# Weighting expert results out of PSUM and storing them in two halves, in a two-layer backbone with 32 experts

## The chip, the core and the metric

One core of one Trainium2 chip. Its engines are TensorE (PE, with weight loads listed apart as PEld), VectorE (DVE), ScalarE (ACT), GpSimd (POOL) and SyncE (SP, which only issues transfers here); 16 DMA engines move data between HBM and SBUF. Each engine executes its own list of instructions in order and waits on semaphores. The metric is the device time of one execution in microseconds, the median of several.

## The reference

Two layers on 256 latent and 256 context tokens of 1024 channels. Each layer has one input projection, three token mixers, a merge and a normalisation, and then a mixture of 32 experts, the part that is changed here. In layer 0 it works on all 512 tokens, in layer 1 on the 256 latent ones.

```python
weights = softmax(top_logit, -1) * group_w          # 2 experts of 32 for each token
def run_block(args):                                # one expert e, some of its tokens
    tok, e = args
    xb = h_pad[tok]
    return (silu(xb @ w1[e]) * (xb @ w3[e])) @ w2[e]    # w1, w3: 1024 x 512, w2: 512 x 1024
y = lax.map(run_block, ...).reshape(cap, d) * slot_w[:, None]
moe = zeros((n_tok + 1, d)).at[slot_tok].add(y)[:n_tok]     # two results for each token
xl = layer_norm(ALPHA * xl + g2_l * moe, ln2_g, ln2_b)      # g2: one row for latent, one for context
```

## The kernel before

A layer's MoE stage has these steps, all written out by the program; only the size of an expert's group of tokens is known at run time.

*Routing and permuting.* Scores, the two experts of each token, its weights `wgt` and its slot `pos` among all slots sorted by expert are computed on DVE, ACT and POOL. `posi` is the slot's row in the DRAM buffer `ysD`, which has two regions: even experts write region 0, odd ones region 1 (NR = 2). `permute(q)` (L1538) builds one-hot matrices `on` for 256 slots (L1544 on DVE and POOL by turns, L1545 on DVE) and PE multiplies the tokens by them (L1551), which gives `XS`, the tokens in slot order, evacuated by DVE (L1555) and ACT (L1557). There are 4 such quarters in layer 0 and 2 in layer 1. Meanwhile POOL scales the residual `X` by the rows of the first normalisation (L1562), which lie in a part of XS that is not used yet.

*Experts.* A block is 64 slots (RB) of one expert. `expert_steps` (L1597) copies the slots to `xt` (L1610), multiplies by w1 and w3 (L1616), takes silu and product (L1621, L1622), transposes (`turn`, L1627), multiplies by w2 (L1636), evacuates 64 slots x 1024 columns, laid out as 128 partitions x 512, to `yo` on ACT (L1638), and POOL stores that with one transfer to ysD (L1639). Expert 0 stands first, between permute(0) and the others: the blocks of its slots 64 to 255 in a nest of three Ifs (L1664), then its slots 0 to 63, then the other permutes, and in layer 0 a loop for more than 256 slots behind an If (L1693). Then experts 1 to 31 follow (L1701 to L1727), software-pipelined: the gate of e stands before the first half of e + 1's up projection. Behind each expert stands an If for over 64 slots (L1721), which holds one block and, in a nested If (L1724), a loop for over 128 slots (L1725); an expert with 64 slots or fewer jumps over both.

*Weights.* Each expert's 6.3 MB come as six pieces of 1 MB on SP's queue into rings (`fetch`, `load_piece`, `reload`). reload(e) at the end of expert e asks for the pieces that take the places of e's own.

*Finish.* POOL gathers the two result rows of each token from ysD (L1738), 8 gathers of 128 rows in layer 0 and 4 in layer 1. ACT multiplies one by its weight (L1742), DVE adds the other with its weight (L1745), POOL (DVE for the last group) multiplies by the gate g2 (L1746), DVE adds ALPHA times the residual (L1747); `normalise` follows for each pair of groups, in layer 1 also the affine part (L387, L388) and the output. Of the weight pieces of layer 1's input projection that are loaded at that time (`raw`), three are issued on ACT behind the third group's scaling (`late`), the rest on SP.

## Time and profile before

| what | value |
|---|---|
| timed runs | 2794.46, 2794.48 and 2802.67 us, median 2794.48 |
| the profiled execution's own time | 2788.21 us |
| its span | 2786.6 us |
| mean granted PE clock | 0.905 of full speed |
| PE busy | 2209.7 us (79%) |
| DVE busy | 1158.0 us (42%) |
| ACT, POOL busy | 664.0 us (24%), 612.6 us (22%) |
| moved by DMA | 657.22 MB, 236 GB/s over the span |
| MoE stage of layer 0, of layer 1 | about 886 to 1538 us, about 2180 to 2787 us |

The profile shows one execution. Busy shares are means over stages with different limits, so a stage is read from windows and from the instructions at its ends, not from the shares of the whole span. The bytes of the two MoE stages are mostly weights: 32 experts of 6.3 MB in each layer.

### The profile page before, as it was taken

To read this page: it belongs to the slowest core of one execution; us is meant where nothing else is said; L and a number is where in the kernel's file an instruction comes from. 1 tells how busy PE (TensorE), PEld (TensorE's weight loads), DVE (VectorE), ACT (ScalarE), POOL (GpSimd) and SP (SyncE) were. 2 spreads that over 40 slices of the span, in tenths; PEclk is the share of its full clock that TensorE was granted. 3 is DMA by queue.
4 is the path that set the end of the run, shared out by engine and by line. 5 is a ranking of instruction groups with operands and counts; after the bars stand their busy time and mean duration, and the time that the engine had idled before them with its cause. 6 is when DMAs were issued, how large, how long until landed. Compare 5 with 4: busy or idle time off the path is not lost. (4 is left out here: it accounts for less than half of the span.)

```text
span 2786.6 us, 42100 instructions
## 1 busy us (share of the span) xinstructions
PE 2209.7 (79%) x16239; PEld 1551.1 (56%) x16239; DVE 1158.0 (42%) x2451; ACT 664.0 (24%) x1308; POOL 612.6 (22%) x542
## 2 busy tenths in 40 slices
PE   7998988888898887777773899986878687678773
PEld 3666975677685644334331576874777443344331
DVE  4749445876456100000003779467864300000002
ACT  2421345443422100000001342345433100000000
POOL 1242110544333000000002242223554200000001
PEclk9998999999999999899887899998988898898886
DMA  9475451323765488999996258343357769999994
GB/s 316 153 215 171 130 167 42 100 76 103 206 213 197 176 345 318 362 408 408 353 382 219 62 164 262 112 154 87 92 167 241 291 248 381 352 400 408 407 389 157
DMA packets 350438, 657.22 MB, mean 236 GB/s; under 512 B 73462, under 2 KB 253214, under 8 KB 306808
## 3 DMA queue, kind: packets, MB, share of 16 engines
q1 hardware_dynamic: 287890, 599.97, 59.4%
q0 software_dynamic: 38160, 24.63, 2.9%
q10 hardware_dynamic: 24022, 27.84, 2.9%
q8 instruction: 218, 3.57, 0.5%
q14 instruction: 148, 1.21, 0.1%
HBM read 593.09 MB, written 59.02 MB: 234 GB/s over the span
## 5 line engine op out<-in xcount | busy, mean ns | idle before, releaser
L1616 PE MATMUL ps<-we,xt 128*64 128x256 f32 x4224 | 569.6, 423 | 240.5 <-PEq L1721 147.4
L1616 PEld LDWEIGHTS ps<-we,xt 128*64 128x64 f32 x4224 | 339.0, 152 | 458.2 <-issue 329.0
L209 PE MATMUL ps<-hT,whi 128*128 128x512 f32 (+2 forms) x880 | 327.1, 372 | 2.1 <-ACT whi L152 1.9
L154 POOL TENSOR_TENSOR wlo<-raw,whi 128x1024 fp32r<-128x1024 f32 (+1 forms) x84 | 206.2, 2455 | 543.6 <-ACT whi L152 453.2
L211 PE MATMUL ps<-hT,wlo 128*128 128x512 f32 (+2 forms) x880 | 317.2, 360 | 0.3 <-DVE wlo L154 0.3
L210 PE MATMUL ps<-hT,whi 128*128 128x512 f32 (+2 forms) x880 | 317.3, 361 | 0.0
L1639 POOL DMA_DIRECT2D ysD<-yo x69 | 55.6, 806 | 1074.7 <-ACT yo L1638 954.0
L1636 PE MATMUL ps<-we,hh 128*64 128x512 f32 x1104 | 251.9, 597 | 5.2 <-DVE hh L1628 2.6
L152 ACT ACTIVATE whi<-raw 128x1024 fp32r<-128x1024 f32 x174 | 180.1, 1044 | 221.9 <-PE ps L210 158.9
L1638 ACT ACTIVATE yo<-ps 128x512 f32<-128x512 f32 x69 | 41.2, 597 | 798.7 <-PE ps L1636 769.9
L1610 DVE COPY xt<-XS 128x512 f32 x66 | 28.2, 427 | 483.2 <-PE ps L1616 479.0
L1628 DVE COPY hh<-ps 128x256 f32<-128x256 f32 x69 | 29.3, 425 | 409.7 <-PE ps L110 409.7
L209 PEld LDWEIGHTS ps<-hT,whi 128*128 128x128 f32 (+1 forms) x880 | 172.0, 195 | 42.4 <-issue 12.6
L211 PEld LDWEIGHTS ps<-hT,wlo 128*128 128x128 f32 (+1 forms) x880 | 171.4, 195 | 31.4 <-issue 6.9
L210 PEld LDWEIGHTS ps<-hT,whi 128*128 128x128 f32 (+1 forms) x880 | 171.9, 195 | 25.0 <-issue 3.3
L154 DVE TENSOR_TENSOR wlo<-raw,whi 128x1024 fp32r<-128x1024 f32 x90 | 148.1, 1647 | 44.6 <-ACT whi L152 38.8
L1636 PEld LDWEIGHTS ps<-we,hh 128*64 128x64 f32 x1104 | 79.5, 138 | 135.2 <-issue 118.8
L210 PE MATMUL ps<-wlo,hT 128*128 128x256 f32 x384 | 110.1, 287 | 1.5 <-DVE wlo L154 1.5
L209 PE MATMUL ps<-whi,hT 128*128 128x256 f32 x384 | 110.9, 289 | 0.0
L211 PE MATMUL ps<-whi,hT 128*128 128x256 f32 x384 | 109.7, 286 | 0.0
L288 PE MATMUL ps<-wmod,sT 128*32 128x256 f32 x768 | 90.0, 521 | 14.0 <-DMA wmod<-in_w_mod 11.5
L1621 ACT ACTIVATE hd<-ps 128x256 f32<-128x256 f32 x69 | 26.4, 383 | 249.9 <-PE ps L1616 249.9
(423 smaller groups left out, 3718.6 us busy)
## 6 DMA issues: line engine op xcount, KB each, us to landing
we<-in_w SPq DMA_DIRECT2D x338, 1024.0 KB
raw<-in_w_in SPq DMA_DIRECT2D x121, 512.0 KB
wmod<-in_w_mod SPq DMA_DIRECT2D x96, 512.0 KB
we<-in_w SPq DMA_DIRECT2D x92, 512.0 KB
ysD<-yo POOLq DMA_DIRECT2D x69, 256.0 KB, 16.2
ysD<-X SPq DMA_DIRECT2D x17, 512.0 KB
raw<-in_w_out SPq DMA_DIRECT2D x16, 512.0 KB
mgD<-st ACTq DMA_DIRECT2D x24, 256.0 KB
```

Of the source, the lines that this page charges most:

```text
L152: nc.scalar.activation(hr[:, :, off:off + pn], rv, AF.Copy)
L154: eng.tensor_sub(lr[:, :, off:off + pn], rv, hr[:, :, off:off + pn])
L209: mm(ps, st[0](k), mv[0](k), start=(k == 0), stop=False)
L210: mm(ps, st[0](k), mv[1](k), start=False, stop=False)
L211: mm(ps, st[1](k), mv[0](k), start=False, stop=(k == kt - 1))
L288: mm(hold["ps"][32 * j:32 * j + 32, :], sT[:, k, :], cols, start=(k == 0), stop=(k == KD - 1 and v not in mod_d[l]))
L1610: nc.vector.tensor_copy(t["xt"], XS[:, :, ds(off, RB)])
L1616: mm(t["ph"][grp[g], i], t["xt"][:, k], (w1, w3)[i](k, g * 256, 256), start=(k == 0), stop=(k == KD - 1), tile_position=(0, g * RB))
L1628: nc.vector.tensor_copy(tl["hh"], pt)
L1636: mm(py[grp[g]], tl["hh"][:, j, grp[f]], w2(k, g * 512, 512), start=(k == 0), stop=(k == 3), tile_position=(0, g * RB))
L1638: nc.scalar.activation(tl["yo"], py, AF.Copy)
L1639: nc.gpsimd.dma_start(ysD[e % NR, ds(off, RB)].rearrange("s (g c) -> g s c", g=2), tl["yo"])
```

## The change

- The result of a block leaves PSUM on DVE, multiplied by the slot's weight (`wc`, one column, two in layer 0: one for each stream) and by the gate row g2; in layer 0 the two streams' products are added. The ACT copy goes.
- The weights of the slots are scattered in slot order to a DRAM buffer `wsD`, with one indirect transfer on POOL for each of the 2 x nb columns (8 in layer 0, 4 in layer 1), and loaded for each block into `wc` by two transfers of 64 rows on POOL, one expert ahead.
- A block's result is stored by two transfers of 64 rows x 512 columns (on POOL, for the last expert on ACT).
- Slots 64 to 127 of an expert are a straight block behind one If. Slots beyond 127 of all experts go to one loop behind one If (`rare`), which stands behind expert 0 in both layers.
- At the end the gathered rows are added to X by plain DVE additions; ALPHA is multiplied into the rows of the first normalisation before (POOL). `normalise` follows all additions.
- The `late` loads are issued on SP with the others. g2 is loaded at the stage's start. The one-hot tiles of permute are single ones in a ring of nb + nst, written in place; hd and hh share a tile.

```diff
-            if late["n"]:
-                late["n"] -= 1
-                with tc.issue_after(late["ins"]):
-                    nc.scalar.dma_start(dst, v)
-            else:
-                nc.sync.dma_start(dst, v)
+            nc.sync.dma_start(dst, v)
...
+        nst = len(streams)
+        wsD = dram.tile([ns + RB, nst], F32, name=f"wsD{l}")
+        g2 = [pe.tile([P, 512], F32, name=f"g2_{s}") for s in streams]
+        for i, s in enumerate(streams):
+            for g in range(2):
+                nc.sync.dma_start(g2[i][g * RB:(g + 1) * RB], mod_d[l][5][s, g * 512:(g + 1) * 512].partition_broadcast(RB))
...
-            on = pr.tile([P, nb, QT], F32R, name="on", tag="on", bufs=2)
+            on = [pr.tile([P, QT], F32R, name="on", tag="on", bufs=nb + nst) for _ in range(nb)]
...
+        nc.gpsimd.tensor_scalar(lnrow, lnrow, ALPHA, None, op0=OP.mult)
...
+        wgt = pr.tile([P, 2, nb, nst], F32, name="wgt")
+        nc.gpsimd.memset(wgt, 0.0)
...
+        nc.scalar.dma_start(wsD[ns:ns + RB], XS[0:RB, 0, ns:ns + nst])
+        for i in range(2):
+            for b in range(nb):
+                nc.gpsimd.indirect_dma_start(out=wsD, out_offset=bass.IndirectOffsetOnAxis(ap=posw[:, i, b:b + 1], axis=0),
+                                             in_=wgt[:, i, b], in_offset=None)
...
+            def weights():
+                for g in range(2):
+                    nc.gpsimd.dma_start(tl["wc"][grp[g]], wsD[ds(off, RB)])
...
-                nc.scalar.activation(tl["yo"], py, AF.Copy)
-                nc.gpsimd.dma_start(ysD[e % NR, ds(off, RB)].rearrange("s (g c) -> g s c", g=2), tl["yo"])
+                for x in range(nst):
+                    nc.vector.scalar_tensor_tensor(tl["hd" if x else "yo"], py, tl["wc"][:, x:x + 1], g2[x], op0=OP.mult,
+                                                   op1=OP.mult)
+                if nst > 1:
+                    nc.vector.tensor_add(tl["yo"], tl["yo"], tl["hd"])
+                last = isinstance(e, int) and e == NE - 1
+                for g in range(2):
+                    (nc.scalar if last else nc.gpsimd).dma_start(ysD[region, ds(off, RB), g * 512:(g + 1) * 512],
+                                                                 tl["yo"][grp[g]])
...
-            with ExitStack() as deeper:
-                for off in range(RB, QT, RB):
-                    deeper.enter_context(tc.If(cnt > off))
-                    expert_block(to, 0, off)
+            with tc.If(cnt > RB):
+                expert_block(to, 0, RB)
...
+        top = nc.values_load(cmax_i, min_val=0, max_val=nt, skip_runtime_bounds_check_because=WHY)
+        with tc.If(top > 2 * RB, label=f"rare{l}", preferred_fallthrough_block=True):
+            with tc.For_i(0, NE, NR) as e0:
+                for x in range(NR):
...
+                    with tc.If(cnt > 2 * RB):
+                        with tc.For_i(2 * RB, cnt, RB) as i:
+                            expert_block(block_tiles(px, *ZO), e, more(off + i), streamed(e), x)
...
+        steps[1][5]()
         steps[1][0]()
...
+                nx[5]()
                 nx[0]()
...
             with tc.If(cnt > RB, label=f"beyond{l}_{e}", preferred_fallthrough_block=True):
-                to = block_tiles(px, *ZO)
-                expert_block(to, e, more(off + RB))
-                with tc.If(cnt > 2 * RB):
-                    with tc.For_i(2 * RB, cnt, RB) as i:
-                        expert_block(to, e, more(off + i))
+                expert_block(block_tiles(px, *ZO), e, more(off + RB))
...
-        g2 = mod_rows(pf, l, 5, streams)
...
-            y0, y1 = yg[b, 0], yg[b, 1]
-            ins = nc.scalar.activation(y0, y0, AF.Copy, scale=wgt[:, 0, b:b + 1])
-            if b == 2:
-                late["ins"] = ins.ins
-            nc.vector.scalar_tensor_tensor(y0, y1, wgt[:, 1, b:b + 1], y0, op0=OP.mult, op1=OP.add)
-            (nc.vector if b == nb - 1 else nc.gpsimd).tensor_mul(y0, y0, g2[(b0 + b) // 2])
-            nc.vector.scalar_tensor_tensor(X[:, b0 + b], X[:, b0 + b], ALPHA, y0, op0=OP.mult, op1=OP.add)
-            if b % 2:
-                normalise([b0 + b - 1, b0 + b])
+            for i in range(2):
+                nc.vector.tensor_add(X[:, b0 + b], X[:, b0 + b], yg[b, i])
+        for b in range(0, nb, 2):
+            normalise([b0 + b, b0 + b + 1])
```

## Rows read from the trace of the kernel before

**Rows 1.** groups by form: the up projection (count, busy, mean ns, idle before, releasers)

```profile
L1616 PE MATMUL ps<-we,xt 128*64 128x256 f32 x4224 | 569.6, 423 | 240.5 <-PEq L1721 147.4 <-DMA we<-in_w 60.4 <-DVE xt L1610 13.9
```

**Rows 2.** line views of L1721, L1693, L1664: branches (count, ns min/median/max, first and last start)

```profile
...
L1721 PEldq COMPARE_BRANCH  x62: 70/3387/7289, 966.8 to 2738.4; - x62
...
L1721 DVEq COMPARE_BRANCH  x62: 50/56/63, 971.1 to 2737.9; - x62
...
L1693 PEldq COMPARE_BRANCH  x1: 362/362/362, 947.2 to 947.2; - x1
...
L1664 PEldq COMPARE_BRANCH  x4: 86/1897/3735, 899.7 to 2190.5; - x4
...
```

**Rows 3.** windows: stretch, length, busy of each engine (instructions), PE clock, DMA share, GB/s

```profile
1066.40:1176.42 110.02, 78.47 (x498) 40.94 (x496) 7.57 (x18) 5.88 (x12) 4.79 (x7) 0.86 0.95 368
1189.26:1303.97 114.71, 85.84 (x578) 45.23 (x576) 8.83 (x21) 6.86 (x14) 5.57 (x7) 0.91 1.02 408
1057.75:1480.05 422.30, 312.60 (x2030) 163.60 (x2032) 30.26 (x72) 24.12 (x49) 19.93 (x26) 0.88 0.97 382
2297.97:2725.00 427.03, 321.14 (x2087) 170.21 (x2084) 31.96 (x76) 24.89 (x51) 20.72 (x26) 0.88 0.99 390
```

**Rows 4.** timeline, end of layer 0's stage (start, us, engine, line, operation, idle before)

```profile
...
1490.22 0.80 POOL L1639 DMA_DIRECT2D ysD<-yo  x1 [9.38 <-ACTq L1721]
...
1500.40 1.07 POOL L1738 DMA_INDIRECT yg<-ysD,posi  x1 [9.38 <-issue]
...
1509.43 0.94 POOL L1738 DMA_INDIRECT yg<-ysD,posi  x1 [0.30 <-issue]
...
1514.96 6.65 DVE L1747 SCALAR_TENSOR_TENSOR X<-X,yg 128x1024 f32<-128x1024 f32 x2
...
1519.27 0.37 ACTq L166 DMA_DIRECT2D raw<-in_w_in  x1
...
1538.07 3.93 PE L110 MATMUL ps<-cst,X 128*128 128x128 f32 x16 [48.83 <-DVE X L384]
...
```

**Rows 5.** timeline, end of layer 1's stage

```profile
...
2743.85 0.80 POOL L1639 DMA_DIRECT2D ysD<-yo  x1 [10.70 <-ACTq L1721]
...
2755.74 1.05 POOL L1738 DMA_INDIRECT yg<-ysD,posi  x1 [11.10 <-DMA ysD<-yo]
...
2773.46 0.21 DVE L378 BATCH_NORM_AGGREGATE bmv<-bst 128x2 f32<-128x12 f32 x1
...
```

**Rows 6.** line views of L1639 and L1738 (landing); transfers of 2735 to 2787, 40 slices

```profile
L1639 POOL DMA_DIRECT2D ysD<-yo x69: 796/796/1077, 913.6 to 2743.8; - x69
...
DMA to landing us min/median/max: 8.6/16.2/21.2
...
DMA to landing us min/median/max: 4.3/5.7/6.5
...
DMA  1012001889711110069988400000000000007920
```

**Rows 7.** timeline of POOL and DVE around expert 0 of both layers

```profile
...
855.06 18.61 POOL L1562 TENSOR_TENSOR X<-X,XS 128x1024 f32<-128x1024 f32 x8 [7.44 <-DMA XS<-in_ln_g]
...
891.53 0.15 DVE L1589 TENSOR_TENSOR wgt<-wgt,e 128x4 f32<-128x4 f32 x1
...
920.94 0.42 DVE L1622 TENSOR_TENSOR hd<-hd,ps 128x256 f32<-128x256 f32 x1 [4.53 <-ACT hd L1621]
...
2188.46 9.30 POOL L1562 TENSOR_TENSOR X<-X,XS 128x1024 f32<-128x1024 f32 x4 [0.61 <-DVE wgt L1588]
...
2211.27 0.69 DVE L1555 COPY XS<-ps 128x512 f32<-128x512 f32 x1 [5.96 <-PE ps L1551]
...
```

**Rows 8.** windows: layer 0 behind expert 0

```profile
935.00:985.00 50.00, 44.79 (x347) 32.20 (x345) 8.20 (x17) 4.69 (x9) 2.61 (x3) 0.97 0.49 190
```

**Rows 9.** groups by form: prices on DVE and POOL

```profile
L1746 DVE TENSOR_TENSOR yg<-yg,mrow 128x1024 f32<-128x1024 f32 x2 | 2.4, 1210 | 0.0
...
L1544 POOL TENSOR_SCALAR o<-io,posq 128x256 f32<-128x256 f32 x10 | 10.1, 1005 | 47.6 <-DVE o L1544 21.4 <-DVE posq L1536 13.7 <-DVE on L1545 11.1
```

More of the change, by code (lines that the diff above doesn't have):

```diff
@@ L156, in split_unit @@
         return hr, lr
-    late = {"n": 0, "ins": None}
     def col_load(src, c0, cn):
@@ L416, in backbone @@
         nq = T - q0
-        late["n"] = 3 if l else 0
         yD = [dram.tile([HID, T], F32, name=f"yD{l}_{i}") for i in range(3)]
@@ L1427, in backbone @@
         cnt_i = pe.tile([1, 2, NE], I32, name="cnt_i")
+        cmax = pe.tile([1, 1], F32, name="cmax")
+        cmax_i = pe.tile([1, 1], I32, name="cmax_i")
+        one_i = pe.tile([1, 2, 1], I32, name="one_i")
         def block_pool(stack, bufs):
@@ L1463, in backbone @@
                    tile_position=(0, 64 * (k % 2)))
-            ls_ = pr.tile([P, CTX], F32, name="ls", tag="o1", bufs=2)
+            ls_ = pr.tile([P, CTX], F32, name="ls", tag="on", bufs=nb + nst)
             nc.vector.tensor_copy(ls_, lT)
@@ L1528, in backbone @@
         nc.vector.tensor_copy(cnt_i, cs_[0:1])
+        nc.vector.tensor_reduce(cmax, cs_[0:1, 0], axis=AX.X, op=OP.max)
+        nc.vector.tensor_copy(cmax_i, cmax)
         pall = pr.tile([P, nb, NE], F32, name="pall", tag="eq", bufs=2)
@@ L1550, in permute @@
                         for x in range(2):
-                            mm(ps[:, i], h2r[(b0 + b) // 2, kp + i][x][:, b % 2], on[:, b], start=(b == 0 and x == 0),
+                            mm(ps[:, i], h2r[(b0 + b) // 2, kp + i][x][:, b % 2], on[b], start=(b == 0 and x == 0),
                                stop=(b == nb - 1 and x == 1))
@@ L1576, in backbone @@
             nc.vector.tensor_add(posi[:, i], pos[:, i], rofs)
+        posw = pr.tile([P, 2, nb], I32, name="posw")
+        nc.vector.tensor_copy(posw, pos)
+        wgt = pr.tile([P, 2, nb, nst], F32, name="wgt")
+        nc.gpsimd.memset(wgt, 0.0)
+        own = [wgt[:, i, 2 * x:2 * x + 2, x] for i in range(2) for x in range(nst)]
         eg = pr.tile([P, nb, NG], F32, name="eg")
@@ L1635, in down @@
                         for g in range(2):
-                            mm(py[grp[g]], tl["hh"][:, j, grp[f]], w2(k, g * 512, 512), start=(k == 0), stop=(k == 3),
+                            mm(py[grp[g]], hh[:, j, grp[f]], w2(k, g * 512, 512), start=(k == 0), stop=(k == 3),
                                tile_position=(0, g * RB))
-                nc.scalar.activation(tl["yo"], py, AF.Copy)
-                nc.gpsimd.dma_start(ysD[e % NR, ds(off, RB)].rearrange("s (g c) -> g s c", g=2), tl["yo"])
-            return rows, up, gate, turn, down
+                for x in range(nst):
+                    nc.vector.scalar_tensor_tensor(tl["hd" if x else "yo"], py, tl["wc"][:, x:x + 1], g2[x], op0=OP.mult,
[6 more added lines that the diff above has]
+                                                                 tl["yo"][grp[g]])
+            return rows, up, gate, turn, down, weights
         def expert_block(*args):
-            rows, up, gate, turn, down = expert_steps(*args)
+            rows, up, gate, turn, down, weights = expert_steps(*args)
+            weights()
             rows()
@@ L1705, in backbone @@
         for e in range(1, NE):
-            rows, up, gate, turn, down = steps.pop(e)
+            rows, up, gate, turn, down, _ = steps.pop(e)
             tc.mark_branch_hint_location(f"beyond{l}_{e}", "LikelyTaken")
```

36 lines of the change are left out of this document (19 added, 17 removed).

## The prediction

> **What bounds the kernel now.** I read four views in this order. The groups of instructions by form first: the costliest group is the up projection of the experts (L1616), and the releaser in front of its idle time is not the weights but PE's own sequencer at L1721, the jump over the second block of an expert: 147.4 of 240.5 us, against 60.4 us for weights that had not landed [rows 1]. Then the line view of L1721: PE meets that branch 62 times, with 70 ns, 3.39 us and 7.29 us as minimum, median and maximum; on DVE the same branch takes 50 to 63 ns. So it is neither the register nor the count that makes it long, but something that PE alone does at that jump [rows 2]. The nearest rows of the same kind are PE's L1693, a jump over a loop that holds one block (0.362 us), and L1664, whose jump over three nested blocks in layer 1 took 3.735 us, its maximum [rows 2].
>
> Third, windows cut at the stores of single experts. 1066.40 to 1176.42 is six experts, and the branch was long in each: 110.02 / 6 = 18.34 us an expert, PE busy 78.47, DMA share 0.95 at 368 GB/s. 1189.26 to 1303.97 is seven experts behind which the branch was short: 16.39 us each, DMA share 1.02 at 408 GB/s [rows 3]. The reader is to see that PE isn't full in either (0.71 and 0.75 of the window), that the DMA queues are full in the second and not in the first, and that therefore the two MoE stages are limited by weights, with PE's stalls making holes in the stream: a PE that stands for 6 to 7 us frees its ring of weight pieces late. That is why 147 us of PE idle time are worth much less than 147 us. Fourth, the two ends of the stages, by timeline: from the last expert's store to PE's restart in layer 0 (1490.22 to 1538.07), and from it to the end of the span in layer 1 (2743.85 to 2786.6). No matmul runs there and each microsecond is on the path [rows 4, 5].
>
> **Part by part.** The sum is made against the profiled execution, 2788.21 us; the median of the timed runs, 2794.48, is 6.3 us above it, and I add that at the end.
>
> *One straight block instead of a nest (stage).* Each expert has about 578 / 7 = 83 matmuls and as many weight loads, 165 PE instructions [rows 3]. The jump at L1721 now crosses two such blocks, the straight one and the one in the loop; after the change it crosses one, like L1693. I take L1693's 0.36 us for it, so the holes go. What is late next is the weights: at 408 GB/s without holes, 1057.75 to 1480.05 shrinks by 422.30 x (1 - 382/408) = 26.9 us and 2297.97 to 2725.00 by 427.03 x (1 - 390/408) = 18.8 us [rows 3]. Sum 45.7; I take **-45**. Bounds: -3, if the stream doesn't fill, and -50.
> [...]
>
> *Tail of layer 0.* Now the store is issued at 1490.22, the first gather at 1500.40, the eighth at 1509.43 (1.29 us apart), and PE restarts at 1538.07, 37.7 us behind the first gather. The adds between run on ACT, DVE and POOL by turns, and beside POOL a DVE operation on X takes 3.3 us (6.65 for two), where the plain 128x1024 one takes 1.21 [rows 4, 9]. After: two stores of 64 rows. The one store of now lands 11 us after issue in layer 1; in its second half, when the loads beside it are through, the DMA share is about a tenth, so most of the engines do nothing for it [rows 5, 6]; a gather of 128 rows of 4 KB lands in 4.3 to 6.5 us [rows 6]. With two stores one behind the other in issue and rows spread over all engines I take 6.5 us, 4 less. Then the last gather is issued 9.0 us behind the first and lands by about 15; the last add is done at about 16.5, statistics and chain of the first pair some 6 to 7: PE restarts about 23.5 behind the first gather, 14 less. Three raw loads of layer 1 no longer wait on ACT (the third was issued at 1519.27), which takes their conversion out of the end of this chain [rows 4]. Of 18 I take **-16**, because ACT's conversions and weight loads may be next; bounds -8 and -20.
>
> *Tail of layer 1.* Store to first gather 11.9 us now; by the same price about 5: -7 (-3 if the second half waits for the first). The gathers run to statistics' end in 17.9 us (2755.74 to 2773.67); after: last gather +3.9, landing 5.3, add 1.21, statistics of two tiles 2.6, about 13.3, -4.5 [rows 5, 6, 9]. **-11**; bounds -6 and -13.
>
> *Small gains.* The nest at L1664 has one level left: some 2 to 3 us in layer 1; the nested If of the four taken experts goes. **-3**, bounds -1 and -5.
>
> *The weights' way (new).* Eight one-column scatters in layer 0 and four in layer 1, each of 128 rows, go out on POOL, then two loads into wc for each block; the STT out of PSUM waits for wc, and behind it on DVE, in order, stand the gate's multiplication and the evacuations of the next permutes. No scatter is in the trace. Lower end of one: 1.25 us, the pace of gathers that don't wait for each other. Upper end: 11 us, if each waits for the landing of the one before as the stores of ysD do [rows 5]. I take 3.6, issue 0.94 and a landing somewhat under the shortest gather's 4.3, since a scatter moves 1 KB. Layer 0: weights known at 891.7, 8 x 3.6, then about 4 for wc: 925; DVE's next needed operation is the gate's at 920.94: +5 [rows 7]. Layer 1: POOL has the affine until 2197.8 and about 6 us of scaling ahead, then 4 x 3.6 and 4: 2222, against an evacuation wanted at 2211: +11. Together **+16**; bounds 0 and +30 for the mechanism of my choice. Nothing covers it: the stages' beginnings have the DMA at 0.49, since the ring is full until PE uses pieces [rows 8]. Further on, wc is asked for an expert ahead, 16 us before its use; free. The STT itself (one or two and an add in place of one ACT copy) lies on a DVE that is busy 8.8 of 115 us [rows 3].
>
> *The rare branch.* Over two blocks, once a layer, taken on PE's path behind expert 0: between L1693's 0.36 and L1721's 7.3; I take 2 each, **+4** (0 to +14). Its body isn't run: the 69 stores are 64 experts and 5 second blocks, and the inner loop's lines have no instruction in the trace [rows 6].
>
> *Scaling of the ln rows.* 128x2048 on POOL: by the affine's 2.33 us for 128x1024 at least 4.7, by L1544's 1.0 us for 128x256 at most 8 [rows 7, 9]. In layer 0 it stands before the affine at 855.06, when DVE routes; it lengthens the stretch in which DVE is slowed: **+3** (0 to +8).
>
> *The permutes' ring.* Six tiles in place of two sets of four: less is made ahead; **+2** (0 to +5). Edits that I cost at nothing: g2 loaded on SP at the stage's start (first needed by expert 0's STT, 50 us later), the merged hd/hh tile (one engine chain orders both already), the fetch's view, cmax.
>
> Sum: -45 -16 -11 -3 +16 +4 +3 +2 = **-50**: 2738.2 for a profiled run, **2745** as a median.
>
> **The rivals.** (a) *The weights are late anyway.* PE's wait moves from the branch to the DMA and the stage gains 3: 2787. For: 60.4 us already wait for weights. Against: 368 beside 408 GB/s in neighbouring windows [rows 1, 3].
> (b) *Half of the long branches stay*, because jump length isn't the cause or one block is still enough: -22 in place of -45, 2767. For: a median of 3.39 shows that middle lengths occur. Against: 0.36 at L1693.
> (c) *Slower: the scatters wait for each other at the store's price.* At 11 us each, layer 0 has wc at 893 + 88 + 4 = 985, +64, layer 1 at 2252, +41: 105 in place of 16, 2834. It decides from 3.6 + 50/12 = 7.8 us a scatter. For: POOL's stores of now do wait for landings, and do take 11 us. Against: that price comes with 256 KB.
> (d) *The halves don't help.* If each half lands like the whole of now, one behind the other, the tails are 22 us of store: 15 and 18 worse, 2778. [...] Against it: the 11 us of now, with the DMA share at a tenth, is no price of a full transfer [rows 5, 6].
>
> **How the numbers follow.** Forecast 0.60; (a) 0.13; (b) 0.12; (c) 0.10; (d) 0.05. The forecast's own terms move it from 2715 (scatters free, tails at their best, -30) to 2770. The range of 8 in 10 takes in (b), (d) and (a): 2715 to 2790. A measurement of this kernel can tell about 0.3%, 8.4 us. Faster by more than that: forecast, (b), (d) and a third of (a), 0.81; within it: the rest of (a), 0.09; slower: (c), 0.10.
>
> **What would show it.** Right: PE's branch behind an expert under 0.5 us everywhere; experts 16.0 to 16.4 us apart and 400 to 408 GB/s through both stages; the first gather 6 to 8 us behind the last store, and PE's restart in layer 1 some 24 us behind it. Wrong: branches of 3 us and more left (b); the stream under 390 GB/s with PE waiting for weights (a); DVE idle for tens of us at expert 0 for wc, scatters 8 us or more apart (c); stores landing after 15 us and more (d). A slower PE clock in the fuller stage would also break it: it was 0.86 and 0.91 in the two windows [rows 3].

## The result and the profile after

The changed kernel took 2722.22 us (median of 4 runs, 2718.27 to 2726.14) beside 2794.47 us of the kernel before: a ratio of 0.973, 95% interval 0.9695 to 0.9765. In a later group of runs (e5_changed, the same kernel) it was 0.9729 (0.9706 to 0.9753). That is 72 to 77 us less; the forecast was 50 less, and the range held the result near its lower edge. Its profiled execution has a span of 2723.5 us, against 2786.6.

I cut both spans at PE's first matmul of expert 0 and its last of expert 31 in each layer, so that the six lengths add up to the span. The line numbers of after are: up projection L1640 (L1616 before), down projection L1659, STT (the scalar_tensor_tensor on DVE that weights a block out of PSUM) L1663, store L1670, wc L1627, scatter L1604, gather L1776, the If behind an expert L1763 (L1721), the rare If L1726.

| us, one profile each | to expert 0 | stage, layer 0 | its end, to PE's restart | layer 1 until expert 0 | stage, layer 1 | its end | span |
|---|---|---|---|---|---|---|---|
| before | 899.9 | 589.4 | 48.8 | 656.8 | 548.0 | 43.7 | 2786.6 |
| changed | 905.9 | 553.9 | 37.9 | 662.6 | 528.0 | 35.2 | 2723.5 |
| changed, second profile (e5_changed) | 903.6 | 555.5 | 38.4 | 658.7 | 531.1 | 35.2 | 2722.5 |

The two stages gave 33.8 to 35.5 and 16.9 to 20.0 us, the ends 10.4 to 10.9 and 8.5. The rest moves by some us from profile to profile.

The up projection's group, which answers to [rows 1] (columns as there):

```profile
L1640 PE MATMUL ps<-we,xt 128*64 128x256 f32 x4224 | 548.4, 412 | 180.3 <-DMA we<-in_w 161.1 <-DVE xt L1634 13.9 <-SPq L1763 3.3
```

The releaser at PE's sequencer is gone, and the weights have taken its place: 161.1 us against 60.4. PE still waits, but for the resource that bounds the stage. The line views of the two Ifs, PE's branch (as [rows 2]):

```profile
L1763 PEldq COMPARE_BRANCH  x66: 70/330/437, 985.4 to 2685.1; - x66
...
L1726 PEldq COMPARE_BRANCH  x2: 1640/2934/4227, 962.9 to 2195.7; - x2
```

All 66 branches behind experts are under 0.44 us, where 33 of 62 had been over 3 us. The rare If costs 1.64 and 4.23 us once a layer. Windows of full stretches of both layers (as [rows 3]):

```profile
1162.10:1305.70 143.60, 111.35 (x742) 58.59 (x740) 30.26 (x54) 3.45 (x9) 18.28 (x35) 0.90 1.02 416
2312.10:2645.50 333.40, 259.55 (x1724) 137.53 (x1722) 42.26 (x84) 8.05 (x21) 44.88 (x86) 0.91 1.02 417
```

416 and 417 GB/s: the stream is full, and faster than the 408 of before's unbroken window. The ends, by timeline (as [rows 4] and [rows 5]):

```profile
1461.94 6.04 ACTq L1670 DMA_DIRECT2D ysD<-yo  x2
...
1471.06 1.06 POOL L1776 DMA_INDIRECT yg<-ysD,posi  x1 [14.47 <-issue]
...
1497.62 3.92 PE L110 MATMUL ps<-cst,X 128*128 128x128 f32 x16 [37.89 <-DVE X L377]
```

```profile
2689.07 5.49 ACTq L1670 DMA_DIRECT2D ysD<-yo  x2
...
2697.47 1.06 POOL L1776 DMA_INDIRECT yg<-ysD,posi  x1 [13.28 <-issue]
...
2710.29 0.21 DVE L371 BATCH_NORM_AGGREGATE bmv<-bst 128x2 f32<-128x12 f32 x1
```

From the first gather to PE's restart it is 26.6 us, from 37.7, and from the first gather to the statistics' end 13.0, from 17.9. But the gather starts 9.1 us behind the issue of the last store in layer 0 and 8.4 in layer 1, only 1.1 and 3.5 us sooner than the 10.2 and 11.9 of before. Line views of the store and the STT say why (the first row: who waited for the store and how long; the last: what the STT's engine waited for):

```profile
  POOL ysD L1670: 348.2, 66
...
DMA to landing us min/median/max: 2.2/5.7/7.5
...
  DMA wc<-wsD: 37.4, 2
```

A store lands in 5.7 us, where it was 16.2 [rows 6]; but the second half waits for the first one's landing, 66 times, 348.2 us of POOL's time. That wait is the program's: in the three blocks of expert 0, whose rows are fixed when the program is written, the second half is issued 0.53 to 0.57 us behind the first (the pair at 931.24 below), and in the 66 others, whose rows are known only at run time, 2.5 to 7.2 us behind it. And DVE stood 37.4 us, twice, for wc. POOL around expert 0 of layer 0, first and last scatter, first store:

```profile
895.59 1.22 POOL L1604 DMA_INDIRECT wsD<-wgt,posw  x1 [1.64 <-DVE wgt L1600]
...
920.49 0.96 POOL L1604 DMA_INDIRECT wsD<-wgt,posw  x1 [1.88 <-DMA wsD<-wgt,posw]
...
931.24 1.06 POOL L1670 DMA_DIRECT2D ysD<-yo  x2 [7.21 <-DVE yo L1666]
```

Seven steps from 895.59 to 920.49 are 3.56 us each on average, the 3.6 of the forecast; one by one they are 2.4 to 6.8 us, since POOL builds one-hot tiles between some of them. Layer 1, POOL and then DVE's STT:

```profile
2155.20 1.11 POOL L1604 DMA_INDIRECT wsD<-wgt,posw  x1 [1.98 <-issue]
...
2175.83 0.96 POOL L1604 DMA_INDIRECT wsD<-wgt,posw  x1 [5.67 <-DMA wsD<-wgt,posw]
...
2176.87 5.37 POOL L1562 TENSOR_SCALAR XS<-XS 128x2048 f32<-128x2048 f32 x1
...
2182.93 9.23 POOL L1566 TENSOR_TENSOR X<-X,XS 128x1024 f32<-128x1024 f32 x4
...
2192.10 0.58 POOL L1627 DMA_DIRECT2D wc<-wsD  x1
...
2194.45 0.75 DVE L1663 SCALAR_TENSOR_TENSOR yo<-ps,wc,g 128x512 f32<-128x512 f32 x1 [25.17 <-DMA wc<-wsD]
```

The transfers in these 20.6 us (columns as in [rows 3]):

```profile
2155.20:2175.83 20.63, 17.93 (x124) 13.09 (x122) 2.71 (x5) 2.86 (x4) 4.07 (x5) 0.92 0.92 296
```

Here a scatter takes (2175.83 - 2155.20) / 3 = 6.9 us, beside the first weights of the stage at 296 GB/s (in layer 0 the scatters had 88 GB/s beside them), and behind the scatters POOL's list has the scaling, one half of wc, the affine of 9.23 us and only then the other half. DVE waited 25.17 us.

### The profile page after: what moved, and what is told of

It is laid out like the page before. It is cut to its first block, busy times and chain, and to the rows that moved or that the text cites. A ratio compares the mean times of both kernels' runs of the same rounds, so it can differ in the third digit from the quotient of the medians.

```text
span 2723.5 us, 42854 instructions
## 1 busy us (share of the span) xinstructions
PE 2202.1 (81%) x16239; PEld 1554.5 (57%) x16239; DVE 1257.1 (46%) x2596; ACT 615.9 (23%) x1233; POOL 713.6 (26%) x757
## 2 busy tenths in 40 slices
DMA packets 325669, 655.09 MB, mean 241 GB/s; under 512 B 48662, under 2 KB 228414, under 8 KB 282136
## 5 line engine op out<-in xcount | busy, mean ns | idle before, releaser
L1640 PE MATMUL ps<-we,xt 128*64 128x256 f32 x4224 | 548.4, 412 | 180.3 <-DMA we<-in_w 161.1
L1640 PEld LDWEIGHTS ps<-we,xt 128*64 128x64 f32 x4224 | 330.6, 148 | 389.1 <-issue 262.7
L1659 PE MATMUL ps<-we,hd 128*64 128x512 f32 x1104 | 251.8, 598 | 4.7 <-DVE hd L1651 4.7
L1670 POOL DMA_DIRECT2D ysD<-yo x134 | 71.4, 533 | 698.1 <-DMA ysD<-yo 348.2
L1663 DVE SCALAR_TENSOR_TENSOR yo<-ps,wc,g 128x512 f32<-128x512 f32 x69 | 51.8, 751 | 374.5 <-PE ps L1659 337.0
L1651 DVE COPY hd<-ps 128x256 f32<-128x256 f32 x69 | 29.3, 425 | 305.2 <-PE ps L110 305.1
L1659 PEld LDWEIGHTS ps<-we,hd 128*64 128x64 f32 x1104 | 78.7, 138 | 135.9 <-issue 120.0
L1627 POOL DMA_DIRECT2D wc<-wsD x138 | 71.7, 520 | 173.2 <-DMA ysD<-yo 71.3
```

Source lines behind the costliest of these rows:

```text
L1627: nc.gpsimd.dma_start(tl["wc"][grp[g]], wsD[ds(off, RB)])
L1640: mm(t["ph"][grp[g], i], t["xt"][:, k], (w1, w3)[i](k, g * 256, 256), start=(k == 0), stop=(k == KD - 1), tile_position=(0, g * RB))
L1651: nc.vector.tensor_copy(hh, pt)
L1659: mm(py[grp[g]], hh[:, j, grp[f]], w2(k, g * 512, 512), start=(k == 0), stop=(k == 3), tile_position=(0, g * RB))
L1663: nc.vector.scalar_tensor_tensor(tl["hd" if x else "yo"], py, tl["wc"][:, x:x + 1], g2[x], op0=OP.mult, op1=OP.mult)
L1670: (nc.scalar if last else nc.gpsimd).dma_start(ysD[region, ds(off, RB), g * 512:(g + 1) * 512], tl["yo"][grp[g]])
```

## The experiments

Each run is compared with the kernel before on the same chip, where its median was 2801.4 to 2801.7 us; the ratios go by that. The runs come in four groups, each on a chip of its own (e1 to e4, e5 to e8, e9 to e11, e12), so that between groups the ratios tell more than the medians. Stage lengths are cut as above, from one profile each; the first table shows by how much they move from one profile to the next.

| run | median us | ratio to before (95%) | stage 0 | end 0 | stage 1 | end 1 |
|---|---|---|---|---|---|---|
| e1_pad | 2767.79 | 0.9890 (0.9873 to 0.9906) | 586.0 | 38.3 | 550.5 | 34.3 |
| e2_hold | 2728.65 | 0.9750 (0.9729 to 0.9771) | 560.1 | 37.5 | 532.6 | 35.3 |
| e3_onestore | 2758.66 | 0.9852 (0.9834 to 0.9870) | 578.0 | 41.4 | 545.6 | 37.5 |
| e4_start | 2699.79 | 0.9639 (0.9623 to 0.9654) | 550.2 | 37.6 | 511.7 | 34.7 |
| e5_changed | 2724.69 | 0.9729 (0.9706 to 0.9753) | 555.5 | 38.4 | 531.1 | 35.2 |
| e6_straight_alone | 2723.03 | 0.9715 (0.9691 to 0.9739) | 552.4 | 49.2 | 518.5 | 44.4 |
| e7_halves_alone | 2767.74 | 0.9873 (0.9850 to 0.9897) | 580.7 | 46.2 | 541.7 | 39.5 |
| e8_late_rare | 2697.70 | 0.9626 (0.9603 to 0.9649) | 547.3 | 37.5 | 514.2 | 35.6 |
| e9_straight_halves | 2700.51 | 0.9633 (0.9608 to 0.9657) | 541.3 | 45.1 | 508.6 | 41.1 |
| e10_straight_halves_late | 2694.70 | 0.9624 (0.9601 to 0.9647) | 538.4 | 46.3 | 504.7 | 42.3 |
| e11_loop | 2733.78 | 0.9759 (0.9738 to 0.9779) | 561.1 | 39.3 | 534.9 | 34.8 |
| e12_pool_first | 2707.21 | 0.9658 (0.9632 to 0.9684) | 555.4 | 37.8 | 514.8 | 36.6 |

The theory after the result had three parts: PE's long branches came from the length of the jump (one); the nest also held the weight pieces of an expert until its second block had ended (two); the old store took bandwidth from the weights (three). A fourth came from the 37.4 us of DVE.

### The jump's length: e1_pad

```diff
                 expert_block(block_tiles(px, *ZO), e, more(off + RB))
+                with tc.If(cnt > 2 * RB):
+                    for z in range(40):
+                        if z % 8 == 0:
+                            pz_ = ps_tile([P, 2, 256])
+                        mm(pz_[0:RB, 0], XS[:, z % 8, 0:RB], XS[:, z % 8, 0:256], start=True, stop=True, tile_position=(0, 0))
```

> The changed kernel with about one block's worth of PE instructions (40 small matrix products, which are never run) behind a nested If in each expert's second block; they read no weights. Theory one, the jump's length makes PE's branch long: 10 to 14 branches of 6 to 7 us come back in each layer, the DMA share falls to 0.92 to 0.95 in those stretches, and the time rises by 20 to 40 us over the changed kernel's 2722, to 2742 to 2762. Rival, the long branches came from the loop and its bookkeeping, not from the length: all branches stay under 0.5 us and the time within 5 us of 2722.

PE's branch behind the experts:

```profile
L1763 PEldq COMPARE_BRANCH  x66: 70/432/6760, 984.6 to 2724.7; - x66
```

The windows of the same kernel, cut where its branches are long (columns as in [rows 3]):

```profile
1349.00:1473.60 124.60, 90.49 (x577) 47.35 (x575) 23.13 (x41) 2.68 (x7) 14.68 (x28) 0.86 0.95 371
2561.80:2684.90 123.10, 90.45 (x576) 47.52 (x574) 14.09 (x28) 2.68 (x7) 14.69 (x28) 0.88 0.99 396
```

Measured: 2767.79, 43 us over e5_changed, a little more than the 20 to 40 expected. 15 branches are over 5 us (27 before; 10 to 14 in each layer were expected), 23 over 3 us (33), in runs, and in one of them the stream is down to 371 GB/s at a share of 0.95, as in [rows 3]. Nothing that is added ever runs, reads weights or holds a piece: theory one is shown, and the loop's bookkeeping is not needed for it. All branches behind experts together are 150.5 us here, 18.8 in e5_changed and 210.9 before: 131.7 us more branch cost 43 us, a third, by the medians, and 50 us by the stages of the two profiles. By these rates before's 192 us are worth 63 to 73 us, an estimate that takes the cost to grow with the branches.

Across one block no branch behind an expert is over 0.5 us (the longest took 437 ns in the changed kernel and 440 ns in e6_straight_alone); across about two, in before and in e1_pad, long ones come in runs. The profile's queue list has a queue of instructions, q8, with 218 packets before, 171 after and 211 with the padding. One long branch of before, and that queue (packets, MB, share of 16 engines) from 1066.9 to 1073.5 us:

```profile
L1721 PEldq COMPARE_BRANCH  x1: 6458/6458/6458, 1067.1 to 1067.1; - x1
...
q8 instruction: 1, 0.02, 1.0%
```

Laid beside all branches, the packets of q8 go with the long ones. During each of the 33 branches over 3 us of before, and of the 23 of e1_pad, just one such packet of 16 KB starts, and the branch ends 1.3 to 1.6 us behind the packet's end; during the 24, 36 and 66 branches under 0.5 us of before, e1_pad and the changed kernel none starts. (Others come between the branches: from 1060 to 1180 us there are 14 packets and seven long branches.) By these numbers PE stands at a long jump until such a packet has come, and in the branches over 5 us it takes 3.4 to 4.8 us until the packet starts. Why one jump has a packet and another none was not shown.

### Pieces held by a nested block: e2_hold and e11_loop

The loop is in e11_loop only; in e2_hold the six products stand in the If itself.

```diff
                 expert_block(block_tiles(px, *ZO), e, more(off + RB))
+                with tc.If(cnt > 2 * RB):
+                    with tc.For_i(2 * RB, cnt, RB) as i:
+                        pz_ = ps_tile([P, 2, 256])
+                        for z in range(6):
+                            mm(pz_[0:RB, 0], XS[:, z, 0:RB], pieces[6 * e + z](0, 0, 256), start=True, stop=True, tile_position=(0, 0))
```

> The changed kernel with a nested If in each expert's second block that holds six small matrix products, one on each of the expert's weight pieces; they are never run, and the jump grows by some 15 PE instructions only. Theory two, a nested block that may read the pieces keeps them until the second block has ended, so that the weight stream stops at the taken experts: behind the five second blocks the stream falls under 200 GB/s for some 15 to 20 us, where the changed kernel has 390 to 417, and the time rises by 15 to 30 us, to 2737 to 2752. Rival, the stream stopped there before because PE was slow in those experts for another reason: the stream stays as in the changed kernel and the time within 5 us of 2722. No long branches by either.

> e2_hold with its six small products on the weight pieces inside a loop, as the second nested block of before had it; never run, and the jump grows by a few tens of PE instructions only. Theory six, it is the loop around the piece readers that stopped the stream at the taken experts: the stretches with second blocks fall to about 200 GB/s for some 18 us, and the time rises by 12 to 25 us over the changed kernel, to 0.978 to 0.982 of before. Rival, the loop adds nothing to e2_hold: 0.974 to 0.975, and the stop of before needs the long jump or the whole second block in it.

SP's waits around the first taken expert of layer 1 (what was waited for; us, times, longest), in e2_hold:

```profile
SPq L1348 <- PEq L1765: 28.4, 1, 28.4
```

and in the changed kernel:

```profile
SPq L1348 <- PE ps L1640: 25.4, 3, 21.5
```

The mechanism is there: SP waits for the nested If's end, 28.4 us at a stretch, where it got a first piece after 21.5. The size was wrong: 4 us for e2_hold, which can't be told from nothing, and 9 for e11_loop, whose interval (0.9738 to 0.9779) just overlaps that of the changed kernel. Cut between the ends of down projections, the stretch of layer 1's first expert with a second block reads, in e2_hold and in e5_changed (columns as in [rows 3]):

```profile
2218.50:2244.10 25.60, 22.46 (x166) 11.94 (x164) 4.04 (x8) 0.77 (x2) 2.63 (x5) 1.00 0.48 182
```

```profile
2213.90:2239.10 25.20, 22.20 (x168) 11.86 (x164) 4.04 (x8) 0.77 (x2) 2.64 (x5) 1.00 0.72 263
```

It gets 182 GB/s in e2_hold and 196 in e11_loop, against 262 and 263 in the two profiles of the changed kernel, but the next expert makes up for it (382 and 316 against 231 and 241). So holding the pieces, as these two runs do it, is worth a few us, not 15 to 30. In before the same stretch got 106 GB/s, and the next 400: a deeper hole than either run makes, and not one of long jumps, since the two branches at L1721 around it took 0.1 and 0.4 us. What the whole nested block of before adds to it was not tried, so theory two is shown as a mechanism and not in its full size.

### The store: e3_onestore and e7_halves_alone

```diff
-                for g in range(2):
-                    (nc.scalar if last else nc.gpsimd).dma_start(ysD[region, ds(off, RB), g * 512:(g + 1) * 512],
-                                                                 tl["yo"][grp[g]])
+                (nc.scalar if last else nc.gpsimd).dma_start(ysD[region, ds(off, RB)].rearrange("s (g c) -> g s c", g=2), tl["yo"])
```

e7_halves_alone makes the opposite edit in the kernel before.

> The changed kernel with the one store of before in place of the two halves (on POOL, for the last expert on ACT). Theory three, the one store costs the weight stream some 9 GB/s through its small packets and lands later: 408 in place of 417 GB/s in the full stretches, some 25000 packets more, 17 us in the two stages, and the first gather 1 to 3 us later in each tail: 2738 to 2746. Rival, packets cost nothing beside the stream and the second half waits for the first anyway: the time within 5 us of 2722.

> The kernel before with the two half stores alone. Theory three: 417 in place of 408 GB/s where the stream is full, but the long branches stay, so half of the 17 us or less shows in the stages; the tails gain 1 to 3.5 us each: 10 to 15 us less than before. Rival, the stores alone are worth what their removal cost in the changed kernel: 30 to 40 us less.

Full stretches of e3_onestore, windows:

```profile
1190.10:1319.70 129.60, 97.84 (x658) 51.69 (x656) 26.91 (x48) 3.07 (x8) 15.43 (x24) 0.91 1.02 407
2330.70:2684.90 354.20, 283.04 (x1808) 148.80 (x1806) 44.35 (x88) 8.45 (x22) 42.19 (x66) 0.92 1.02 408
```

Packets of e3_onestore, then of the changed kernel:

```profile
DMA packets 354550, 655.29 MB, mean 237 GB/s; under 512 B 77547, under 2 KB 257299, under 8 KB 311021
```

```profile
DMA packets 325669, 655.09 MB, mean 241 GB/s; under 512 B 48662, under 2 KB 228414, under 8 KB 282136
```

407 and 408 GB/s at the same DMA share of 1.02: the queues are as full, with 28885 more packets under 512 B, and carry 9 GB/s less. Theory three has its rate and its place. The page's list of queues has the price by itself: POOL's queue q0 (packets, MB, share of 16 engines) in e6_straight_alone and in e9_straight_halves below, which differ in the store alone:

```profile
q0 software_dynamic: 38160, 24.63, 3.1%
```

```profile
q0 software_dynamic: 8160, 23.86, 2.4%
```

3.1% of 2721.6 us are 84 us of all 16 engines and 2.4% of 2701.5 are 65, so the old store takes 19 us more of them, 18 of these in packets under 512 B; the two stages differ by 21 us. But the time rose by 34 us, not 16 to 24, and e7_halves_alone gained 34, which is its rival's 30 to 40, where I had expected 10 to 15 from the store in a stream that still has holes. For e3_onestore one more cost is seen; its STT waited for wc:

```profile
  DMA wc<-wsD: 67.7, 5
```

five times and 67.7 us instead of 37.4: three times at expert 0 (49.6 us) and at two later blocks (8.1 and 10.0). Part of the 34 us may lie there; why these waits are longer was not shown. For e7_halves_alone its profile shows only -8.7, -2.7, -6.3 and -4.2 us in stages and ends, and 15 us in the whole span; the rest of its 34 lies between the profiles and the timed runs, since before's own profile is 6 to 13 us under its medians and e7's 5 over its own. So how much of the 34 the stages hold stays open.

### One block, alone and with the halves: e6_straight_alone, e9_straight_halves, e5_changed

e6_straight_alone puts this part alone into the kernel before (with the rare loop, its maximum count and the fetch's view as in the change; the lines here show the two Ifs), e9_straight_halves adds the two stores; weights and gate stay at the end, on ACT, DVE and POOL.

```diff
-            with ExitStack() as deeper:
-                for off in range(RB, QT, RB):
-                    deeper.enter_context(tc.If(cnt > off))
-                    expert_block(to, 0, off)
+            with tc.If(cnt > RB):
+                expert_block(to, 0, RB)
...
-                to = block_tiles(px, *ZO)
-                expert_block(to, e, more(off + RB))
-                with tc.If(cnt > 2 * RB):
-                    with tc.For_i(2 * RB, cnt, RB) as i:
-                        expert_block(to, e, more(off + i))
+                expert_block(block_tiles(px, *ZO), e, more(off + RB))
```

> The kernel before with the straight block and the one rare loop alone (the weighting, the store and the end stay as before). Theory one and two: all of PE's branches behind experts are under 0.5 us, the full stretches run at 408 GB/s, and the stream no longer stops at the five taken experts: 45 us from the branches, 15 to 25 from the taken experts, 3 to 6 lost to the rare branch: 55 to 65 us less than before. Rival, the stop at the taken experts belongs to the old store: only 40 us less, and 200 GB/s or less stays behind the second blocks.

> The kernel before with the straight block and rare loop and with the half stores, and with nothing else of the change: the results are still weighted and gated at the end. Theory five, the two parts add up (0.9715 and 0.9873 alone) and weighting out of PSUM has cost the changed kernel more than it gave: 0.958 to 0.962 of before, some 30 to 40 us under the changed kernel's 0.973; expert 0's blocks as short as in e6_straight_alone, the full stretches at 417 GB/s. Rival, the gains overlap, since both fill the same stream: 0.968 to 0.973.

> The changed kernel as it is, beside the runs of this group, so that the others can be compared with it on the same chip: 0.973 of the kernel before, as in the first comparison; each theory says the same.

The straight block alone gives 79 us by the medians (65 between the two profiles), as much as the whole change and more than the 55 to 65 expected: its stages are 37.0 and 29.5 us shorter, its ends as before. Windows of it, two full stretches and the two beginnings, from PE's first matmul of expert 0 to the end of the ninth block of layer 0 and of the seventh of layer 1:

```profile
1158.20:1305.40 147.20, 115.30 (x741) 59.79 (x739) 11.37 (x27) 8.83 (x18) 7.18 (x9) 0.92 1.02 410
2325.30:2647.50 322.20, 256.35 (x1644) 135.49 (x1642) 25.29 (x60) 19.63 (x40) 15.98 (x20) 0.92 1.02 410
893.77:1043.10 149.33, 136.06 (x995) 87.72 (x997) 19.81 (x45) 12.90 (x24) 10.30 (x14) 0.97 0.69 266
2158.66:2256.90 98.24, 87.92 (x640) 52.79 (x642) 11.04 (x25) 8.30 (x16) 9.46 (x8) 0.97 0.77 292
```

the beginnings of before, to the end of the same blocks:

```profile
899.87:1056.80 156.93, 134.76 (x994) 85.81 (x994) 19.73 (x43) 13.49 (x25) 10.22 (x14) 0.97 0.62 241
2194.87:2297.00 102.13, 88.85 (x640) 51.63 (x642) 10.67 (x24) 7.46 (x15) 7.86 (x8) 0.97 0.67 257
```

The full stretches run at 410 GB/s, as the forecast had it. The beginnings are what it left out: the same blocks end 7.6 us sooner in layer 0 and 3.9 in layer 1, and by then 39.7 MB have come instead of 37.8, and 28.7 instead of 26.2. Before's beginnings hold one long jump of PE, 3.60 us at L1664 in layer 0, and two second blocks behind experts in each layer; the branches at L1721 took 0.07 to 0.43 us there. What each of these is worth was not told apart. The stream starts the full stretch with about 2 MB more in hand. From these blocks to the end of the stages it gains another 29.4 and 25.7 us.

With the halves in addition the full stretches of e9_straight_halves read:

```profile
1151.00:1300.00 149.00, 113.74 (x774) 60.19 (x770) 12.20 (x29) 9.82 (x20) 9.94 (x19) 0.92 1.02 418
2317.70:2640.00 322.30, 250.10 (x1674) 133.06 (x1672) 25.27 (x60) 20.23 (x41) 21.45 (x41) 0.90 1.01 418
```

418 GB/s. Its stages are 11.1 and 9.9 us shorter than those of e6_straight_alone, its ends 4.1 and 3.3; the ratio is 0.9633, and the rival of 0.968 to 0.973 is out, though the gains overlap a little (0.9592 would be the product). So both kernels that lack the weighting out of PSUM do at least as well as the change: what the rest of the change adds on top, from e9_straight_halves to e5_changed, is +14.2 and +22.5 us in the stages and -6.7 and -5.9 in the ends. Nearly all of the loss lies at expert 0, where wc is first waited for: between the ends of the down projections of its two blocks in layer 0 it is 27.1 us instead of 13.0, and from its block to expert 1's in layer 1 45.0 instead of 25.8.

### What the weighting costs: e4_start, e8_late_rare, e10_straight_halves_late, e12_pool_first

```diff
-        nc.gpsimd.tensor_scalar(lnrow, lnrow, ALPHA, None, op0=OP.mult)
+        nc.scalar.activation(lnrow, lnrow, AF.Copy, scale=ALPHA)
...
-                    nc.gpsimd.dma_start(tl["wc"][grp[g]], wsD[ds(off, RB)])
+                    (nc.sync if isinstance(off, int) else nc.gpsimd).dma_start(tl["wc"][grp[g]], wsD[ds(off, RB)])
```

> The changed kernel with two moves at the stage's start: the ln rows are scaled on ACT in place of POOL, and expert 0's wc is loaded on SP in place of POOL. Theory four, the wait of DVE for wc in expert 0 (12 us in layer 0 and 25 us in layer 1) is on the path, and in layer 1 it is POOL's scaling and affine (5.4 and 9.2 us) that stand before the loads: wc some 10 us earlier in layer 1 and 3 us earlier in layer 0, the time 8 to 15 us lower, 2707 to 2714. Rival, the stage is bound by weights and makes the delay up: the time within 4 us of 2722.

e4_start is 25 us under e5_changed (0.9639), more than either theory: 5.3 us in layer 0's stage and 19.4 in layer 1's. It has two moves at once, and their shares were not told apart. The last scatter and the affine of layer 1:

```profile
2159.73 0.96 POOL L1604 DMA_INDIRECT wsD<-wgt,posw  x1 [1.98 <-DMA wsD<-wgt,posw]
...
2161.87 9.37 POOL L1566 TENSOR_TENSOR X<-X,XS 128x1024 f32<-128x1024 f32 x4 [1.17 <-DMA yg<-ysD,posi]
```

From the first scatter (2146.92) to the last it is 12.8 us, where the changed kernel took 20.6, and the affine follows at once, 15.0 us behind the first scatter instead of 27.7. A likely reason for the quicker scatters is in the DMA windows and in SP's waits (columns as in [rows 3]; who waited for what: us, times, longest):

```profile
2153.19:2156.70 3.51, 3.51 (x37) 2.80 (x33) 0.48 (x1) 1.77 (x1) 1.92 (x2) 1.00 0.13 35
2156.70:2159.73 3.03, 2.54 (x24) 1.69 (x20) 0.04 (x1) 1.81 (x3) 1.05 (x1) 1.00 0.01 0
...
SPq L1627 <- DMA wsD<-wgt,posw: 14.7, 1, 14.7
```

SP now stands 14.7 us for the scatters before it may load wc, and the weights behind that load on its list wait too. So the last steps of the scatters, 3.5 and 3.0 us, run beside 35 and 0 GB/s, while the first one, beside 334 GB/s, took 6.3. So the second move may work in part by clearing the queues. I had counted DVE's wait alone. The affine also bounds the stage: the ln rows lie in the part of XS that the last permute writes, so that what makes POOL late makes expert 1 late.

e8_late_rare moves the rare If of e4_start behind the last expert, e10_straight_halves_late that of e9_straight_halves:

```diff
-        top = nc.values_load(cmax_i, min_val=0, max_val=nt, skip_runtime_bounds_check_because=WHY)
-        with tc.If(top > 2 * RB, label=f"rare{l}", preferred_fallthrough_block=True):
...
             reload(e)
+        top = nc.values_load(cmax_i, min_val=0, max_val=nt, skip_runtime_bounds_check_because=WHY)
+        with tc.If(top > 2 * RB, label=f"rare{l}", preferred_fallthrough_block=True):
```

> The kernel of e4_start with the rare If moved behind the last expert, where PE has nothing to do. Theory: PE's branch there of 1.6 and 4.2 us was on the path behind expert 0, where the weights' ring is full: 4 to 6 us less than e4_start, 0.962 of before. Rival, PE would wait for expert 1's slots in that time anyway, or the branch is as long for the engines that the gathers need: within 3 us of e4_start.

> e9_straight_halves with the rare If behind the last expert as in e8_late_rare. Theory: PE's branch of 1.6 to 4.2 us behind expert 0 goes, 2 to 6 us less than e9_straight_halves. Rival, as e8_late_rare has shown so far, no difference that can be told: within 3 us.

0.9626 after 0.9639, and 0.9624 after 0.9633: both go the way of the theory, by 4 and 3 us, and neither difference is clear of its interval. What the rare If is worth can't be told from nothing.

```diff
+                if isinstance(off, int):
+                    nc.scalar.activation(tl["yo"], py, AF.Copy)
+                    for x in range(nst - 1, -1, -1):
+                        z = tl["hd" if x else "yo"]
+                        nc.gpsimd.tensor_scalar(z, tl["yo"], tl["wc"][:, x:x + 1], None, op0=OP.mult)
+                        nc.gpsimd.tensor_mul(z, z, g2[x])
+                    if nst > 1:
+                        nc.gpsimd.tensor_add(tl["yo"], tl["yo"], tl["hd"])
```

> The kernel of e8_late_rare in which expert 0's blocks are evacuated by ACT unweighted, as before the change, and weighted and gated by POOL from SBUF, so that nothing but POOL waits for wc; all other experts as in the changed kernel. Theory seven, what the weighting cost is DVE's wait for wc in expert 0, and nothing else: DVE has no wait for wc left, expert 0's blocks take as long as in e9_straight_halves (12.9 and 41.7 us in layer 0, 25.8 in layer 1, from the end of one down projection to the next), and with the shorter ends of the changed kernel the time is 8 to 14 us under e8_late_rare, 0.957 to 0.960 of before. Rival, the weighting costs through the scatters and the two loads of each expert as well: 0.962 to 0.964, as e8_late_rare and e9_straight_halves.

DVE has no wait for wc any more, and yet the kernel is not faster: 0.9658, with an interval that overlaps that of e8_late_rare, and in the one profile layer 0 is back at 555.4. Its waits in expert 0 of layer 0 (who, for whom: us, times, longest):

```profile
ACT hd L1644 <- POOL yo L1669: 7.3, 1, 7.3
```

and in layer 1, behind expert 0:

```profile
DVE XS L1558 <- POOL X L1566: 14.0, 2, 10.1
```

In layer 0 the second block and the first of expert 0 share the tiles hd and yo, so that the first block's gate waits for POOL's last operation on them. In layer 1 the evacuation of the last permute waits for POOL's affine. So theory seven fails: it wasn't DVE's wait as such. By these waits, whoever waits for wc in expert 0 holds tiles, or POOL, for which the next step waits; the run also gives POOL the weighting to do, and the two aren't told apart. Whether the scatters' own pace could be cut (all rows are disjoint, yet POOL stood 29.6 us, 9 times in the changed kernel, for the landing of the scatter before) was not tried.

## Why the prediction was right, and where it was not

The direction, the bound and the main term's mechanism were right: the time fell by 72 to 77 us, inside 2715 to 2790, and it fell because PE's jumps got short and the weights' stream has no holes. The forecast was 22 to 27 us short of it. Of its signs, the branches came as written; the experts were 15.9 us apart at 416 and 417 GB/s, both a little better; the first gather, 9.1 and 8.4 us behind the last store instead of 6 to 8, and PE's restart, 26.6 us behind it instead of 24, were missed; and DVE's 25 us of waiting for wc at expert 0 was written as a sign of (c). By its own steps:

- *Stage, -45.* The mechanism is shown (e1_pad, e6_straight_alone); the term measured 66.5 us. The step that failed is the pair of windows: 1057.75 to 1480.05 and 2297.97 to 2725.00 began where the stream was already full. Ahead of them PE had one long jump (3.60 us at L1664, layer 0) and two second blocks behind experts in each layer, and the DMA moved only 241 and 257 GB/s. 11.5 us of the 21 that are missing were won there; behind them the stages gave 55 us instead of 45, through 410 GB/s and through what was already in hand. I had used the idle DMA of the beginnings [rows 8] only to say that nothing covers the weights' way, not as time to be won.
- *The halves, costed in the ends only.* Missing term: 21 us in the two stages, through 408 to 417 GB/s. The old store's small packets were in the page's count (73462 under 512 B, 48662 after); the forecast priced its landing and not what it takes from the others.
- *End of layer 0, -16:* measured -10.4 to -10.9. The adds came out about as worked out, 26.6 us from gather to restart (23.5 forecast, 37.7 before). The store did not: I had taken two stores one behind the other in issue, but the second waits for the first's landing (it is issued 5.6 us behind it there), and three DVE operations now stand before it.
- *End of layer 1, -11:* measured -8.5. Gather to statistics 13.0 (13.3 forecast). Store to gather 8.4, which is the bound that I had written for a second half that waits (-3).
- *The weights' way, +16:* measured +14.2 and +22.5 in the stages, 37 together, above my upper bound of 30; it holds the other small edits of the change too, but 33 of it lie where wc is first waited for. The pace of layer 0 was right on average, 3.56 us. In layer 1 it was 6.9, and I had put wc's loads behind the affine as a whole in time, but not the affine behind the scatters in front of the last permute (e4_start).
- *Rare If, +4:* 1.64 and 4.23 us on PE, and some 3 to 4 us in the time that can't be told from nothing. *Scaling, +3:* 5.37 us on POOL in the range of 4.7 to 8; e9_straight_halves, without it, reaches expert 0 of layer 0 at 904.0 as e5_changed does at 903.6, so there it cost nothing that can be seen; in layer 1 it stands between the scatters and the affine, a part of the loss above that e4_start takes out. *Permutes' ring, +2:* from expert 0's end to expert 1's it is 41.3 us in e5_changed and 41.7 in e9_straight_halves; nothing.
- *The rivals.* (a) and (b) are out: PE waits for weights, but at 417 GB/s, and the longest branch behind an expert is 0.44 us. (c) had the right place and, at 3.6 and 6.9 us a scatter, less than its price of 11; POOL's order added to it. (d) is out as well: a half lands in 5.7 us. The halves do wait for each other, but by the program's own order, as expert 0's pairs show: 0.53 to 0.57 us from issue to issue, where the 66 others have 2.5 to 7.2. For this form of store the two halves are 34 us faster than the one transfer (e3_onestore, e7_halves_alone).

So -66.5 -21 -10.4 -8.5 +37 = -69, which is what stages and ends of the two profiles show (1229.9 to 1160.2); the span differs by 64, since the other parts are 5.6 us longer in this profile. Against the forecast's -50 the missing term and the loss that was 21 too small cancel, which is luck, the ends gave 8 less and the small terms 6 less of a loss; what is left is the main term, 21 too small.

Open: by e1_pad's rates 63 to 73 us are the branches', beside the 66.5 that e6_straight_alone shows in its stages and the 79 of its medians. The pieces' early release is worth some us (4 and 9 in e2_hold and e11_loop, neither clear), but before's stream fell lower at the taken experts than theirs does; how the term divides between the two has not been told apart.

## What to carry to other kernels

When an engine's stall makes holes in a stream that bounds the stage, price it by the stream, over the whole stage, its ramp included, and look for what else rides on the same queues: here the form of a store was worth 21 us in the stages, more than each of the ends. A wait that is moved onto a new chain (scatter, load, use) has to be followed through every list and every shared tile that its engines serve, not only to its first user. And a part that pays can hide one that doesn't: the straight block and the half stores alone, 0.9633, are better than the whole change, 0.973, and no run here is clearly faster than they are (0.9624 with the rare If moved).

## What was not expected of the hardware

- With some 29000 more packets under 512 B, at the same 655 MB in all, the stream fell from 417 to 408 GB/s at the same DMA share of 1.02 (e3_onestore against the changed kernel; e6_straight_alone at 410 against e9_straight_halves at 418, with 18 us of all 16 engines in these packets).
- Each of PE's 56 branches over 3 us (33 before, 23 in e1_pad) ended 1.3 to 1.6 us behind the end of one 16 KB packet of the instruction queue; 131.7 us more of branches cost 43 us of time (e1_pad against e5_changed): a third, in a stage that is bound by weights.
- The scatter of 128 rows took 3.56 us from issue to issue in layer 0, beside 88 GB/s, and 6.9 us in layer 1, beside 296 GB/s; with the weights held back (e4_start, 35 and 0 GB/s) it took 3.5 and 3.0 us there.
